# Eight-stage transformer kernel on one core: stage joints' transposes placed further back, tail weights in buffers of their own, and the end of the convolution stage rearranged

## The chip, the cores and the metric

The kernel runs on one core of one Trainium2 chip. The metric is device microseconds (us) of one execution, the median of several runs. The engines are named as in the profile: PE is TensorE, DVE VectorE, ACT ScalarE, POOL GpSimd, and SP the engine that only issues transfers here.

## The reference, cut to what matters

Two blocks work on one sequence of 256 tokens with 1024 features in fp32. Each has two mixers, and a SwiGLU feed-forward part behind each mixer: eight stages of the form `x = x + f(rms_norm(x))`.

```python
def rms_norm(x, w):
    xf = x.astype(jnp.float32)
    y = xf * lax.rsqrt(jnp.mean(xf * xf, axis=-1, keepdims=True) + NORM_EPS)
    return (y * w.astype(jnp.float32)).astype(x.dtype)
...
def swiglu(h, w_gate, w_up, w_down):
    return (jax.nn.silu(h @ w_gate) * (h @ w_up)) @ w_down
...
def conformer_conv(h, w_pw1, b_pw1, w_dw, b_dw, ln_g, ln_b, w_pw2, b_pw2):
    a, gate = jnp.split(h @ w_pw1 + b_pw1, 2, axis=-1)
    u = a * jax.nn.sigmoid(gate)
    dw = lax.conv_general_dilated(
        u, w_dw[:, None, :], window_strides=(1,), padding=((CONV_WIDTH_2 - 1, 0),),
        dimension_numbers=('NWC', 'WIO', 'NWC'), feature_group_count=D_MODEL) + b_dw
    d32 = dw.astype(jnp.float32)
    mu = jnp.mean(d32, axis=-1, keepdims=True)
    var = jnp.mean(jnp.square(d32 - mu), axis=-1, keepdims=True)
    z = (d32 - mu) * lax.rsqrt(var + EPS) * ln_g + ln_b
    z = jax.nn.silu(z).astype(h.dtype)
    return z @ w_pw2 + b_pw2
```

The mixers are, in order, a state-space and gated-linear-attention layer, a latent attention (called mla), a retention layer with pooling, and the convolution stage above (conformer), with 31 taps for each feature.

## The kernel before

**Precision.** Each fp32 product is made of three: every operand is split in a part `hi` (a cast, on ACT) and a rest `lo` (a subtraction, on DVE), and PE adds hi by hi, hi by lo and lo by hi. `load` does this for a piece of weights: fetch `raw` by DMA, four casts (L159), four subtractions (L160). `split` does it for activations (L164 on ACT, L165 on DVE).

**A stage.** `x` lies as two tiles of 128 tokens, t0 and t1. The last step of a stage is `outproj`: it takes weights in chunks of two times 128 rows, and keeps the last two chunks as a tail that it runs in four groups of 12 matmuls of 512 columns: t0 first half, t0 second half, t1 first half, t1 second half. When a group is done, DVE adds it to `x` (L382) and ACT squares that half (L274). After the second half of a tile DVE, POOL (`r`, a power of -1/2, L227) and DVE again (`xn`, L291) make the normed tile, PE transposes it in eight 128 by 128 pieces (`transposes`, L251), ACT casts the transpose from PSUM to `xT` hi (L164), and DVE subtracts for `xT` lo (L165). The next stage multiplies by `xT`.

**Joints.** The passage from one stage to the next is called a joint here; there are seven, 1 to 7. Code is written stage by stage, and a scheduler sets each engine's order by priorities: `high_priority(offset=FIRST)` brings an instruction forward, `issue_after` holds it behind another. In a joint PE runs the transposes of t0 inside the last group of the old stage, and those of t1 inside the first matmuls of the new stage, which work on t0's tokens.

**The convolution stage (joint 6 to joint 7).** `proj(i)` makes four slices of the gated input, `conv(ks)` the taps. Most taps run on PE: for each tap and 128 features two diagonal matrices (hi and lo) are made by ACT (`diags`, L1095: identity times a column of the weights `whl_dw`), and three matmuls of 256 columns (L311 to L313) use them. The other taps run on DVE. Then follow, for all features, the statistics (`stat`: transposes L1204, bn_stats, bn_aggr), POOL's power (`lnr`, L1225), eight broadcast matmuls in PSUM (L1229), a multiply and an add on DVE (L1235, L1236), SiLU on ACT, a split to `zTh` and `zTl`, and `outproj` with `conv_w_pw2`, whose bias `bp` is added to `x` on DVE (L1242).

Of the kernel before, what the change touches and what calls it, by code (L numbers as in the profile page):

```python
# [17 lines left out]
P = 128  # L18
D = 1024
# [38 lines left out]
class Net:  # L58
    def __init__(self, tc, a, ctx):
# [3 lines left out]
        self.entry = []  # L63
        pool = lambda name, bufs, **kw: ctx.enter_context(tc.tile_pool(name=name, bufs=bufs, **kw))
# [81 lines left out]
    def load(self, srcs, k, n, ahead=None, pieces=None, raw=None):  # L146
# [61 lines left out]
    def warm(self, n):  # L208

        b = self.bank("pw", (P, P))  # L210
        for i in range(n):
            self.nc.tensor.matmul(b, self.ones, self.ones, start=True, stop=True)
# [83 lines left out]
    def norm_T(self, t, gain, xn=None, ssq=None):  # L296
        xn = self.normed(t, gain, xn, ssq)
        self.last_norm = self.rs.ins
        self.transposes(xn, self.xT[0][:, :, T(t)], self.xT[1][:, :, T(t)], D)
        self.last_xT = self.last_hi, self.last_lo  # L300


    def mm3A(self, out, lh, ll, wh, wl, first, last):
        mm = self.nc.tensor.matmul
        mm(out, lh, wh, start=first, stop=False)  # L305
        mm(out, lh, wl, start=False, stop=False)  # L306
        mm(out, ll, wh, start=False, stop=last)  # L307
# [13 lines left out]
    def projA(self, w, evac, n=512, tok=(0, 1)):  # L321
# [4 lines left out]
        for t in tok:  # L326
            b = self.bank("acc")
            for k in range(8):
                hi, lo = ch[k // kc]
                self.mm3A(b[:, :n], xh[:, k, T(t)], xl[:, k, T(t)], hi[:, k % kc, :], lo[:, k % kc, :], k == 0, k == 7)  # L330
# [14 lines left out]
    def outproj(self, w, lhs, ks, after, tail=2, ahead=None, pieces=None):  # L345
# [5 lines left out]
        def mms(c, t, hi, lo, hs=(0, 1)):  # L351
            for j in range(2):
                lh, ll = lhs(ks[2 * c + j], t)
                st, sp = c == 0 and j == 0, c == nch - 1 and j == 1
                for h in hs:
                    cs = slice(h * 512, h * 512 + 512)
                    b = banks[t][h]
                    nc.tensor.matmul(b, lh, hi[:, j, cs], start=st, stop=False)  # L358
                    nc.tensor.matmul(b, lh, lo[:, j, cs], start=False, stop=False)  # L359
                for h in hs:  # L360
                    cs = slice(h * 512, h * 512 + 512)
                    nc.tensor.matmul(banks[t][h], ll, hi[:, j, cs], start=False, stop=sp)  # L362
# [994 lines left out]
```

## Time and profile before

| | |
|---|---|
| median of 3 runs | 1308.64 us (1308.57 to 1309.65) |
| profiled execution | 1307.43 us |
| its span, first to last instruction | 1305.4 us |
| PE busy | 1272.3 us, 97% of the span |
| DVE busy | 913.7 us, 70% |
| ACT busy | 780.6 us, 60% |
| POOL busy | 47.7 us, 4% |
| mean granted PE clock | 0.995 |

The span is 2.0 us shorter than the profiled execution's time: that much lies before the first and behind the last instruction. The profiled execution is 1.2 us below the median. A time in a row of the trace counts from the start of the span. A busy share is an average over stages that are limited in different ways, so the sections below go by stretches.

### The profile page before, as it was taken

How to read it: one execution, taken by the hardware profiler on the slowest of the kernel's cores; microseconds unless marked ns; L12 is line 12 of the kernel's file. 1: busy time of each engine (PE TensorE's matmuls, PEld its weight loads, DVE VectorE, ACT ScalarE, POOL GpSimd, SP SyncE). 2: the span in 40 equal slices, each digit the busy share in tenths (PEclk: the TensorE clock that was granted, in tenths of full speed). 3: DMA queues.
4: the chain of work that ended last, by engine and by line, in shares of the span. 5: the costliest groups of instructions: out<-in, count | busy, mean ns of one | idle time of the engine just before them, and what ended most of it. 6: DMA issues, size and time to landing. Idle time of an engine off the chain costs nothing.

```text
span 1305.4 us, 19252 instructions
## 1 busy us (share of the span) xinstructions
PE 1272.3 (97%) x7148; PEld 1090.7 (84%) x7148; DVE 913.7 (70%) x1884; ACT 780.6 (60%) x1794; POOL 47.7 (4%) x103
## 2 busy tenths in 40 slices
PE   9999999999999999999999999999999997999997
PEld 8888877888888867888887887888889996888886
DVE  6966666777746887866746787776548997776643
ACT  6773554666644876666644445666439995666642
POOL 3000000300000000000000000000000000000000
PEclk9999999999999999999999999999999998999999
DMA  8436344766553432766554545555665204555561
GB/s 251 144 119 208 129 181 148 221 194 194 194 193 137 166 97 87 237 194 194 194 194 163 202 137 190 179 181 179 220 194 163 88 11 156 183 182 179 188 220 38
DMA packets 150543, 219.62 MB, mean 168 GB/s; under 512 B 6634, under 2 KB 119426, under 8 KB 150450
## 3 DMA queue, kind: packets, MB, share of 16 engines
q1 hardware_dynamic: 148528, 213.43, 50.4%
q0 software_dynamic: 1920, 4.96, 1.4%
q8 instruction: 56, 0.92, 0.3%
q14 instruction: 37, 0.30, 0.1%
q10 hardware_dynamic: 2, 0.00, 0.0%
HBM read 217.33 MB, written 1.05 MB: 167 GB/s over the span
## 4 chain that ended last, share of the span: by engine, by line
PE 86%; DVE 7%; ACT 3%; issue 2%; POOL 1%; DMA 1%; POOLq 0%; DVEq 0%; ACTq 0%
PE acc L318 18%; PE acc L319 9%; PE acc L358 8%; PE acc L359 8%; PE acc L362 8%; PE pw L318 5%; PE acc L307 4%; PE acc L305 4%; PE acc L306 4%; DVE lo L160 3%; PE pw L319 2%; PE acc L313 2%; PE acc L312 2%; PE acc L311 2%; PE ptr L251 2%
## 5 line engine op out<-in xcount | busy, mean ns | idle before, releaser
L160 DVE TENSOR_TENSOR lo<-raw,hi 128x512 fp32r<-128x512 f32 (+2 forms) x800 | 515.7, 683 | 194.8 <-ACT hi L159 192.5
L159 ACT CAST hi<-raw 128x512 fp32r<-128x512 f32 (+2 forms) x800 | 448.8, 616 | 247.4 <-PE acc L362 101.1
L318 PE MATMUL acc<-xT,hi 128*128 128x512 f32 x1024 | 361.6, 398 | 0.0
L319 PE MATMUL acc<-xT,lo 128*128 128x256 f32 x1024 | 287.6, 281 | 0.0
L318 PEld LDWEIGHTS acc<-xT,hi 128*128 128x128 f32 x1024 | 192.3, 188 | 46.7
L319 PEld LDWEIGHTS acc<-xT,lo 128*128 128x128 f32 x1024 | 193.4, 189 | 0.2
L359 PE MATMUL acc<-lo,hTh 128*128 128x512 f32 x352 | 137.3, 390 | 0.0
L358 PE MATMUL acc<-hi,hTh 128*128 128x512 f32 x352 | 137.3, 390 | 0.0
L362 PE MATMUL acc<-hi,hTl 128*128 128x512 f32 x352 | 113.6, 389 | 0.0
L305 PE MATMUL acc<-hi,xT 128*128 128x512 f32 (+2 forms) x288 | 108.3, 376 | 0.0
L307 PE MATMUL acc<-hi,xT 128*128 128x512 f32 (+2 forms) x288 | 108.0, 375 | 0.0
L306 PE MATMUL acc<-lo,xT 128*128 128x512 f32 (+2 forms) x288 | 107.7, 374 | 0.0
L423 DVE TENSOR_TENSOR s<-s,acc 128x256 f32<-128x256 f32 x128 | 53.3, 417 | 52.7 <-ACT s L422 52.6
L318 PE MATMUL pw<-xT,hi 128*128 128x512 f32 x256 | 90.2, 397 | 0.0
L313 PE MATMUL acc<-xT,lo 128*128 128x256 f32 x288 | 81.9, 284 | 0.0
L311 PE MATMUL acc<-xT,hi 128*128 128x256 f32 x288 | 81.8, 284 | 0.0
L312 PE MATMUL acc<-xT,hi 128*128 128x256 f32 x288 | 81.8, 284 | 0.0
L358 PEld LDWEIGHTS acc<-hi,hTh 128*128 128x128 f32 x352 | 66.1, 188 | 13.7
L362 PEld LDWEIGHTS acc<-hi,hTl 128*128 128x128 f32 x352 | 66.1, 188 | 13.6
L359 PEld LDWEIGHTS acc<-lo,hTh 128*128 128x128 f32 x352 | 66.1, 188 | 13.6
L422 ACT COPY s<-acc 128x256 f32<-128x256 f32 x128 | 47.3, 370 | 45.2 <-PE acc L319 45.2
L319 PE MATMUL pw<-xT,lo 128*128 128x256 f32 x256 | 71.8, 281 | 0.0
(429 smaller groups left out, 2003.6 us busy)
## 6 DMA issues: line engine op xcount, KB each, us to landing
raw<-w_in_even SPq DMA_DIRECT2D x22, 1024.0 KB, 5.3
raw<-w_down SPq DMA_DIRECT2D x22, 1024.0 KB, 5.0
raw<-ffn_w_down SPq DMA_DIRECT2D x22, 1024.0 KB, 5.0
raw<-w_gate SPq DMA_DIRECT2D x20, 1024.0 KB, 5.4
raw<-w_up SPq DMA_DIRECT2D x20, 1024.0 KB, 5.4
raw<-ffn_w_gate SPq DMA_DIRECT2D x20, 1024.0 KB, 5.3
raw<-ffn_w_up SPq DMA_DIRECT2D x20, 1024.0 KB, 5.4
raw<-conv_w_pw SPq DMA_DIRECT2D x12, 1024.0 KB, 5.2
```

What stands on the lines that cost most here:

```text
L159: nc.scalar.copy(fl(hi)[:, c], fl(raw)[:, c])
L160: nc.vector.tensor_sub(fl(lo)[:, c], fl(raw)[:, c], f32(fl(hi)[:, c]))
L305: mm(out, lh, wh, start=first, stop=False)
L306: mm(out, lh, wl, start=False, stop=False)
L307: mm(out, ll, wh, start=False, stop=last)
L311: mm(out, wh, xh, start=first, stop=False)
L313: return mm(out, wl, xh, start=False, stop=last).ins
L318: mm(out.rearrange("p a s -> p (a s)"), wh, self.xx[:, k].rearrange("p a s -> p (a s)"), start=first, stop=False)
L319: mm(out[:, 0, :], wl, self.xx[:, k, 0, :], start=False, stop=last)
L358: nc.tensor.matmul(b, lh, hi[:, j, cs], start=st, stop=False)
L359: nc.tensor.matmul(b, lh, lo[:, j, cs], start=False, stop=False)
L362: nc.tensor.matmul(banks[t][h], ll, hi[:, j, cs], start=False, stop=sp)
```

## The change

**Joints.** `norm_T` now returns a function that does the transposes. `outproj` calls it for t0 behind the fourth matmul of the last group (`done[3]`), and leaves t1's to the next stage, which calls it in `second` behind its 23rd of 24 matmuls on t0 (feed-forward and retention stages), its 40th of 48 (mla) or its 44th of 48 (conformer). The casts of the two loads that follow are held behind the joint (`self.hold`).

**Own tail buffers.** `own=True` in the two feed-forward stages ahead of mla and of the conformer puts the tail chunks' hi and lo into the stage's own pool, so that the buffers of the common pool `whl` are free for the next stage's weights before the joint.

**Convolution stage.** The split of the tap weights `whl_dw` moves behind the joint. The 16 diagonals of the first eight taps of the last 128 features (k = 7) are made by one POOL instruction. Products on a constant matrix of ones, whose results nobody reads, run after the last statistics transposes (`warm(10, "ptr")`) and after the broadcast matmuls (`warm(7, "ptr")`). Of the output weights' pieces the first four casts come ahead of ACT's last 20 diagonals, and DVE's subtractions for the next are held behind given steps.

```diff
-    def load(self, srcs, k, n, ahead=None, pieces=None, raw=None):
+    def load(self, srcs, k, n, ahead=None, pieces=None, raw=None, pool=None):
...
-        hi = self.whl.tile([P, k, n], F32R, tag="hi", name="hi")
-        lo = self.whl.tile([P, k, n], F32R, tag="lo", name="lo")
-        with self.tc.high_priority(offset=ahead):
+        hi, lo = [(pool or self.whl).tile([P, k, n], F32R, tag=t, name=t, bufs=2 if pool else None) for t in ("hi", "lo")]
+
+        whole, parts = self.hold.pop(0) if self.hold else ((), ())
+        with self.tc.high_priority(offset=ahead), ExitStack() as st:
+            for ins in whole:
+                st.enter_context(self.tc.issue_after(ins))
...
-                nc.vector.tensor_sub(fl(lo)[:, c], fl(raw)[:, c], f32(fl(hi)[:, c]))
+                with self.tc.issue_after(parts[i]) if parts else nullcontext():
+                    nc.vector.tensor_sub(fl(lo)[:, c], fl(raw)[:, c], f32(fl(hi)[:, c]))
...
+    def behind(self, ins, turn):
+
+        with self.tc.high_priority(offset=FIRST), self.tc.issue_after(ins):
+            turn()
+
+    def second(self, mms, n):
+
+        if self.turn_xT:
+            self.behind(mms[min(n, len(mms)) - 1], self.turn_xT)
+            self.turn_xT = None
+
+            self.joint = self.last_hi, self.last_lo
+            self.hold = [(self.joint, ())] * 2
...
-                after(t, xn, ssq)
...
+                turn = after(t, xn, ssq)
+            if t == 0:
+                turn0 = turn
+            elif turn:
+                self.behind(done[3], turn0)
+                self.turn_xT = turn
...
+                        self.second(mms, 23)
...
-            self.outproj(wd, lambda k, t: (hTh[:, k, T(t)], hTl[:, k, T(t)]), list(range(NC)), after)
+            self.outproj(wd, lambda k, t: (hTh[:, k, T(t)], hTl[:, k, T(t)]), list(range(NC)), after, pool=sp if own else None)
...
+                self.second(mms, 40)
...
+        if k == 7 and taps[0] == 0:
+
+            n = len(taps)
+            w = self.whl_dw[:, 0, :n, :, k].rearrange("p a b -> p (a b)").rearrange("p (a o) -> p a o", o=1).to_broadcast([P, 2 * n, P])
+            self.nc.gpsimd.affine_select(t[:, :2 * n], w, pattern=[[0, 2 * n], [1, P]], base=0, channel_multiplier=-1, compare_op=ALU.is_equal, fill=0.0)
+            return t
...
+                        self.second(mms, 44)
...
+                if ks[0] == 0:
+                    with self.tc.issue_after(self.joint[0]), self.tc.issue_after(self.joint[1]):
+                        for i in range(2):
+                            n = 16 - i
+                            self.split(self.whl_dw[:, i, :n, 0], self.whl_dw[:, i, :n, 1], self.wdw[:, i::2])
...
+                with self.tc.issue_after(turned):
+                    self.warm(10, "ptr")
...
+                with self.tc.issue_after(ins):
+                    self.warm(7, "ptr")
...
-            self.outproj(a["conv_w_pw2_2"][0], lambda k, t: (zTh[:, k, T(t)], zTl[:, k, T(t)]), list(range(8)), after, ahead=1)
+
+            self.hold = [((), ()), ((), (eps, eps, adds[1], adds[2])), ((), (adds[3],) * 4)]
+            self.outproj(a["conv_w_pw2_2"][0], lambda k, t: (zTh[:, k, T(t)], zTl[:, k, T(t)]), list(range(8)), after, ahead=1, ahead0=120)
```

How the order of instructions changes is shown at three places. A row is a line of the code, the operation, output and inputs, and the shape; `xN` is a number of equal instructions in a row.

PE in joint 1 before: the last group of the old stage is `acc<-..,mT`, the new stage's matmuls on t0 are `acc<-..,xT`.

```order
L359 MATMUL acc<-lo,mT_1477 128x512
L362 MATMUL acc<-hi,mT_1478 128x512
L251 MATMUL ptr<-ident,xn 128x128 x4
L358 MATMUL acc<-hi,mT_1477 128x512
L251 MATMUL ptr<-ident,xn 128x128 x4
L359 MATMUL acc<-lo,mT_1477 128x512
L362 MATMUL acc<-hi,mT_1478 128x512
...
L306 MATMUL acc<-lo,xT 128x512
L307 MATMUL acc<-hi,xT 128x512
L251 MATMUL ptr<-ident,xn 128x128 x8
L305 MATMUL acc<-hi,xT 128x512
L306 MATMUL acc<-lo,xT 128x512
```

The same place of the changed kernel:

```order
L389 MATMUL acc<-hi,mT_1478 128x512
L385 MATMUL acc<-hi,mT_1477 128x512
L258 MATMUL ptr<-ident,xn 128x128 x8
L386 MATMUL acc<-lo,mT_1477 128x512
L389 MATMUL acc<-hi,mT_1478 128x512
...
L330 MATMUL acc<-hi,xT 128x512
L330 MATMUL acc<-lo,xT 128x512
L258 MATMUL ptr<-ident,xn 128x128 x8
L331 MATMUL acc<-hi,xT 128x512
L330 MATMUL acc<-hi,xT 128x512
L330 MATMUL acc<-lo,xT 128x512
L331 MATMUL acc<-hi,xT 128x512
```

The transposes of t0 moved from the border of the last group to behind four of its 12 matmuls, and those of t1 from behind 18 to behind 23 of the new stage's 24 matmuls on t0, so that one of these is left behind them and t1's own matmuls follow.

ACT at the end of the convolution stage, before:

```order
L1173 CAST uh_10750<-uh 128x285
L1174 CAST ul_10751<-ul 128x285
L1095 ACTIVATE diag<-ident,whl_dw 128x128 x36
L159 CAST hi<-raw 128x512 x12
L1238 ACTIVATE d<-d,lp 128x256
L164 CAST zTh<-d 128x256
```

And of the changed kernel:

```order
L1140 ACTIVATE diag<-ident,whl_dw 128x128 x13
L164 CAST hi<-raw 128x512 x2
L1222 CAST uh_10750<-uh 128x285
L164 CAST hi<-raw 128x512
L1223 CAST ul_10751<-ul 128x285
L164 CAST hi<-raw 128x512
L1140 ACTIVATE diag<-ident,whl_dw 128x128 x20
L164 CAST hi<-raw 128x512 x8
```

Sixteen diagonals left ACT, and four of the twelve casts of output weights that stood behind the last diagonal stand ahead of the last 20.

DVE in joint 6, of the changed kernel; `xT` here is lo, `x_82` and `x_83` are t0 and t1 of `x`:

```order
L411 TENSOR_TENSOR x_83<-x_83,acc 128x512
L294 SCALAR_TENSOR_TENSOR v_9510<-ssq_9504,v_9509 128x1
L298 SCALAR_TENSOR_TENSOR xn<-x_83,r,gain 128x512 x2
L1298 TENSOR_TENSOR x_82<-x_82,bp 128x1024
L1298 TENSOR_TENSOR x_83<-x_83,bp 128x1024
L171 TENSOR_TENSOR xT<-ptr,xT 128x4x128 x2
L166 TENSOR_TENSOR lo<-raw,hi 128x512 x4
```

Before, the two adds of `bp` stood behind t1's `xT` and behind the subtraction for `whl_dw`; now they stand between t1's `xn` and its `xT`. The transfer of `bp`, on SP's queue, waits in both kernels for a matmul that last reads what lay in its place: before for one of the retention stage, now for the sixth matmul of the last group of the stage ahead (the second behind t0's transposes).

## Rows read from the trace of the kernel before

**Rows 1.** Page, part 1: busy time and share of the span by engine.

```profile
PE 1272.3 (97%) x7148; PEld 1090.7 (84%) x7148; DVE 913.7 (70%) x1884; ACT 780.6 (60%) x1794; POOL 47.7 (4%) x103
```

**Rows 2.** TensorE's waits over the span: us in total, times, longest.

```profile
PE ptr L251 <- DVE xn L291: 7.7, 16, 0.6
```

**Rows 3.** TensorE timeline, joint 1: start, duration, in brackets idle before.

```profile
217.49 0.39 PE L362 MATMUL acc<-hi,mT 128*128 128x512 f32 x1
217.72 0.39 PE L358 MATMUL acc<-hi,mT 128*128 128x512 f32 x1
...
219.82 0.63 PE L251 MATMUL ptr<-ident,xn 128*128 128x128 f32 x4 [0.58 <-DVE xn L291]
...
228.13 1.29 PE L251 MATMUL ptr<-ident,xn 128*128 128x128 f32 x8 [0.40 <-DVE xn L291]
```

**Rows 4.** VectorE timeline, joint 1.

```profile
221.11 0.69 DVE L165 TENSOR_TENSOR xT<-ptr,xT 128x512 fp32r<-128x512 f32 x1 [0.17 <-ACT xT L164]
...
223.02 1.29 DVE L160 TENSOR_TENSOR lo<-raw,hi 128x512 fp32r<-128x512 f32 x2
224.23 0.68 DVE L382 TENSOR_TENSOR x<-x,acc 128x512 f32<-128x512 f32 x1
```

**Rows 5.** GpSimd timeline, joint 6 and the end of the convolution.

```profile
978.67 0.56 POOL L227 TENSOR_TENSOR r<-v,nhalf 128x1 f32<-128x1 f32 x1 [176.60 <-DVE v L287]
...
1080.04 1.08 POOL L1225 TENSOR_TENSOR lnr<-rm,nhalf 128x2 f32<-128x2 f32 x1 [90.24 <-DVE rm L1224]
```

**Rows 6.** Windows: us, busy of each engine, TensorE clock, DMA share, GB/s.

```profile
988.00:1076.00 88.00, 87.59 (x714) 86.49 (x714) 83.19 (x196) 87.48 (x269) 0.58 (x1) 1.00 0.27 90
1069.00:1076.40 7.40, 7.40 (x48) 6.53 (x47) 4.75 (x13) 7.40 (x26) 0.00 (x0) 1.00 0.01 2
...
1081.00:1091.00 10.00, 7.30 (x20) 5.92 (x21) 8.96 (x19) 6.83 (x13) 0.12 (x1) 0.50 0.64 210
```

**Rows 7.** ScalarE timeline, joint 6.

```profile
987.43 0.49 ACT L164 CAST whl_dw<-wdw 128x128 fp32r<-128x128 f32 x2
987.83 0.98 ACT L1095 ACTIVATE diag<-ident,whl_dw 128x128 fp32r<-128x128 f32 x3
```

**Rows 8.** ScalarE timeline, end of the convolution.

```profile
1065.62 10.65 ACT L1095 ACTIVATE diag<-ident,whl_dw 128x128 fp32r<-128x128 f32 x36
1076.18 3.20 ACT L159 CAST hi<-raw 128x512 fp32r<-128x512 f32 x6
```

**Rows 9.** VectorE timeline, end of the convolution.

```profile
1076.74 0.42 DVE L1198 TENSOR_TENSOR d<-d,pw 128x256 f32<-128x256 f32 x1 [2.99 <-PE pw L313]
...
1078.54 0.63 DVE L160 TENSOR_TENSOR lo<-raw,hi 128x512 fp32r<-128x512 f32 x1
...
1083.29 0.42 DVE L1235 TENSOR_TENSOR d<-d,pw 128x256 f32<-128x256 f32 x1 [0.76 <-PE pw L1229]
1083.63 0.68 DVE L160 TENSOR_TENSOR lo<-raw,hi 128x512 fp32r<-128x512 f32 x1
```

**Rows 10.** TensorE timeline, end of the convolution.

```profile
1077.22 0.44 PE L1204 MATMUL ptr<-ident,d 128*128 128x128 f32 x2 [0.52 <-DVE d L1198]
1081.18 1.22 PE L1229 MATMUL pw<-ident,lnr 128*128 128x128 f32 x4 [3.52 <-POOL lnr L1225]
...
1085.77 0.80 PE L358 MATMUL acc<-hi,zTh 128*128 128x512 f32 x1 [2.52 <-ACT zTh L164]
1086.36 0.63 PE L359 MATMUL acc<-lo,zTh 128*128 128x512 f32 x1
1086.79 0.63 PE L358 MATMUL acc<-hi,zTh 128*128 128x512 f32 x1
```

**Rows 11.** DMA issues from 974 to 984: KB, median us from issue to landing.

```profile
bp<-conv_b_pw SPq DMA_DIRECT2D x1, 512.0 KB, 6.2
```

**Rows 12.** VectorE timeline: the two adds of the convolution's last bias.

```profile
992.24 2.35 DVE L1242 TENSOR_TENSOR x<-x,bp 128x1024 f32<-128x1024 f32 x2
```

**Rows 13.** TensorE timeline, start of the kernel: products on ones.

```profile
1.10 4.63 PE L212 MATMUL pw<-ones 128*128 128x128 f32 x20 [1.10 <-POOL ones L88]
```

More of the change, by code (lines that the diff above doesn't have):

```diff
@@ L1 @@
 import math
-from contextlib import ExitStack
+from contextlib import ExitStack, nullcontext
 import numpy as np
@@ L206, in load_x, with warm @@
         return gain
-    def warm(self, n):
-        b = self.bank("pw", (P, P))
+    def warm(self, n, tag="pw"):
+        b = self.bank(tag, (P, P))
         for i in range(n):
-            self.nc.tensor.matmul(b, self.ones, self.ones, start=True, stop=True)
+            ins = self.nc.tensor.matmul(b, self.ones, self.ones, start=True, stop=True).ins
+        return ins
     def gain(self, g, eng=None):
@@ L298, in norm_T, with turn @@
         self.last_norm = self.rs.ins
-        self.transposes(xn, self.xT[0][:, :, T(t)], self.xT[1][:, :, T(t)], D)
-        self.last_xT = self.last_hi, self.last_lo
+        xh, xl = self.xT
+        def turn():
+            self.transposes(xn, xh[:, :, T(t)], xl[:, :, T(t)], D)
+        return turn
+    def behind(self, ins, turn):
[4 more added lines that the diff above has]
+            self.behind(mms[min(n, len(mms)) - 1], self.turn_xT)
+            self.turn_xT = None
+            self.joint = self.last_hi, self.last_lo
+            self.hold = [(self.joint, ())] * 2
     def mm3A(self, out, lh, ll, wh, wl, first, last):
         mm = self.nc.tensor.matmul
-        mm(out, lh, wh, start=first, stop=False)
-        mm(out, lh, wl, start=False, stop=False)
-        mm(out, ll, wh, start=False, stop=last)
+        return [mm(out, lh, wh, start=first, stop=False).ins, mm(out, lh, wl, start=False, stop=False).ins,
+                mm(out, ll, wh, start=False, stop=last).ins]
     def mm3W(self, out, wh, wl, xh, xl, first, last):
@@ L343, in projW, with outproj @@
         return ins
-    def outproj(self, w, lhs, ks, after, tail=2, ahead=None, pieces=None):
+    def outproj(self, w, lhs, ks, after, tail=2, ahead=None, pieces=None, pool=None, ahead0=None):
         nc = self.nc
@@ L366, in outproj @@
             k0 = ks[2 * c]
-            hi, lo = self.load([w[k0 * P:(k0 + 2) * P, :]], 2, D, ahead, pieces=pieces if c < 2 else None)
+            hi, lo = self.load([w[k0 * P:(k0 + 2) * P, :]], 2, D, ahead0 if ahead0 and c == 0 else ahead, pieces=pieces if c < 2 else None, pool=pool if c >= nch - tail else None)
             if c < nch - tail:
@@ L1108, in conformer @@
             self.whl_dw = pp.tile([P, 2, 16, 2, 8], F32R, name="whl_dw")
-            for i in range(2):
-                n = 16 - i
-                self.split(self.whl_dw[:, i, :n, 0], self.whl_dw[:, i, :n, 1], self.wdw[:, i::2])
             with self.tc.issue_after(self.last_norm):
@@ L1180, in conv @@
                             ts = taps[odd][t0:t0 + 8]
-                            dg = self.diags(pp, ts, k)
+                            with self.tc.issue_after(self.joint[0]):
+                                dg = self.diags(pp, ts, k)
                             for n, tap in enumerate(ts):
@@ L1228, in conformer @@
                     for t in range(2):
-                        nc.tensor.matmul(br[:, i, T(t)], x[:, t, :].to_broadcast([P, P]), self.ident, start=True, stop=True)
-            k = 0
+                        ins = nc.tensor.matmul(br[:, i, T(t)], x[:, t, :].to_broadcast([P, P]), self.ident, start=True, stop=True).ins
+                with self.tc.issue_after(ins):
+                    self.warm(7, "ptr")
+            k, adds = 0, []
             for w in (1, 1, 2, 2, 2):
```

52 lines of the change are left out of this document (32 added, 20 removed).

## The prediction, made before the changed kernel ran

> **What bounds the kernel now.** I read the page's first part: TensorE is busy for 97% of the span, so time can only be won where it pauses, where it is paced by another engine, or where its clock is low [rows 1]. The view of its waits says where it pauses: the largest entry is its wait for the normed tile `xn` ahead of the transposes, 16 times, 7.7 us together [rows 2]. Two of these stand at the kernel's start with 1.0 us; the other 14 are the two pauses of each of the seven joints, 6.7 us or 0.48 us each. The slot lost is longer than the pause shown: a 512-column matmul is drawn 0.39 us long but the next starts after 0.227 us, so 0.16 us of each pause lies under the last matmul's drawn end [rows 3]. That makes 0.64 us a pause, 1.29 us a joint, 9.0 us in all. This is the most that the joints can give.
>
> The windows show a second place. From joint 6 to the last tap ScalarE is busy for 87.5 of 88.0 us, so this stretch is as long as ScalarE's list of work; TensorE looks as busy, but near the end its matmuls are spread out by the diagonals they wait for. After it, from 1081 to 1091, TensorE's granted clock is 0.50, its 1.2 GHz level, where it is 1.00 before [rows 6]. It fell after TensorE had waited 3.52 us for POOL's power, and stayed down while it waited 2.52 us more for `zTh` [rows 10].
>
> **Joints, t0.** The transposes come four matmuls later, 4 x 0.227 = 0.91 us, against a slot of 0.64 to 0.75 us that was lost (0.58 + 0.16 in joint 1) [rows 3]. `xn` is then there; I leave 0.05 us. What follows them, the new stage's first matmul on `xT`, comes 8 x 0.227 = 1.8 us behind the eight transposes, and the first half of `xT` lo is there 221.11 + 0.69 - 219.82 = 1.98 us after they start [rows 3, 4], against 1.0 + 1.8 = 2.8 us: no new wait.
>
> **Joints, t1.** With T the start of t0's transposes, TensorE reaches t1's at T + 1.0 (eight transposes) + 1.8 + 23 x 0.227 = T + 8.0. In joint 1 one subtraction of 0.64 us still stands ahead of t1's last add to `x`; this add then starts at about 3.2 + 0.64 = T + 3.8 (223.02 less 219.82 and one of the two subtractions), and from its start to the transposes before it were 228.13 - 224.23 = 3.9 us [rows 3, 4]: ready at T + 7.7, or T + 8.2 if ScalarE's square waits behind a cast. I take 0.1 us of pause, bounds 0 and 0.3. A new wait follows: only one matmul of t0 is left behind t1's transposes, and t1's third matmul wants `xT` lo at 1.0 + 3 x 0.227 = 1.7 us, when it is there after 1.98 us. So 0.3 us, bounds 0.1 and 0.8 (the chain on ScalarE and VectorE late by a subtraction). Behind the waiting matmul stands the whole queue of TensorE.
>
> A joint so gives 1.29 - 0.05 - 0.1 - 0.3 = 0.84 us (bounds 0.3 and 1.2); five of them (1, 3, 4, 5, 7) 4.2 us. In joint 2 (mla) eight matmuls are left behind t1's transposes, and with own tail buffers no subtraction stands in the chain: 1.2 us. Sum 5.4 us. Joint 6 gives nothing, since ScalarE bounds what follows.
>
> **Joint 6 to the last tap.** ScalarE's list behind joint 6 changes as follows. Sixteen diagonals go to POOL, but three were made inside the joint before [rows 7], so 13 x 0.296 = 3.8 us less (10.65 us for 36); eight casts more (four of a load that is now held behind the joint, four of the output weights ahead of the last 20 diagonals), 8 x 0.533 = 4.3 us (3.20 us for six) [rows 8]; and the split of `whl_dw`, 0.45 us of 0.49 [rows 7]. The last diagonal comes 0.9 us later. Bounds: 0, if ScalarE finds its half microsecond of idle time and joint 6 ends earlier; 2.6 with the next paragraph.
>
> The adds of `bp`, 2.35 us [rows 12], now stand on VectorE ahead of t1's `xT` lo. Their transfer waits for the second matmul behind t0's transposes, T + 1.0 + 0.45, and landed 6.2 us after issue before [rows 11]: T + 7.65. The adds then last to T + 10.0. T1's transposes come at T + 1.0 + 1.8 + 44 x 0.114 = T + 7.8 (a 256-column matmul at half of 0.227), and `xT` lo would start 1.3 us later, at T + 9.1 [rows 3, 4]. TensorE waits some 0.9 us for it. ScalarE next needs TensorE's result behind eight held casts, the `whl_dw` split and some diagonals, over 5 us, so I cost this at nothing; if the transfer lands 1.7 us later still, that cover is gone, and 1.7 us goes onto the chain.
>
> **POOL's diagonals.** No row shows so wide a select. Below, nothing: POOL has idled for 90 us ahead of its power [rows 5]. Above, as slow as ScalarE's sixteen, 4.7 us, hidden while they are asked for late. I take nothing. POOL's power took 0.56 us with VectorE idle and 1.08 us with subtractions beside it [rows 5]. The Trainium skill, "SBUF — State Buffer", section "Who interferes with whom", says that a VectorE instruction with two SBUF inputs and a GpSimd instruction that reads SBUF lock each other out for a whole instruction; the two durations agree. By that rule VectorE would stand still for the whole select; the rival below prices this.
>
> **End of the convolution.** VectorE's subtractions between the two bn_aggr and the epsilon go, 2 x 0.54 us from start to next start (0.63 us long): 1.1 us. The broadcast matmuls took from 1081.18 to VectorE's multiply at 1083.29, 2.1 us at the lower clock; at the upper half of that: 1.05 us. The subtraction between the first multiply and add (0.68 us, 0.6 to the add) goes [rows 9, 10]. The output projection so starts 2.7 us earlier after the last tap. Its matmuls start every 0.43 us, against 0.227, until about 1091.1: 13 of them, 13 x 0.20 = 2.6 us [rows 3, 10]. Together 5.3 us; less 0.9 us by which the last tap is late: 4.4 us. All that rests on the clock rests on the products on ones. Ten took 4.63 us at the start of the kernel [rows 13], at the lower level; half of that, 2.3 us, fits the pause, which is 1.1 us shorter than 3.52 now. Bounds: all 5.3 us, and -1.4 us (first rival). The Trainium skill, "TensorE: Matmul & The Clock Gate", Part 1, says that the gate looks at recent activity and that the lower clock is the default; this trace agrees (0.50 behind the pause), but whether products on a constant count as activity here no row shows beyond the kernel's start.
>
> **Sum.** 5.4 + 4.4 = 9.8 us off the profiled execution's 1307.43 us: 1297.6. That execution is 1.2 us below the median of 1308.64 us, to which the forecast is put: **1298.8 us**.
>
> **Rivals.**
> - *The clock falls all the same* (TensorE also waits about 2 us for the last 20 diagonals, behind the four casts). The ten products then last 4.63 us from 1077.7 to 1082.3, the broadcast ends at 1084.4, 1.1 us behind that of before; less 0.6 us for the subtraction. With the 0.9 us: -1.4 us, total 5.4 - 1.4 = 4.0: 1304.6. For it: it fell here before. Against: ten products fill the wait.
> - *T1's transposes only turn into waits for `xT` lo*, 0.8 us in five joints instead of 0.3 and 0.1: 2.0 us less, 1300.8; with the `bp` transfer late too, 1302.5. For it: one matmul of cover. Against: with the loads held, VectorE has nothing else to do there.
> - *Slower: the stretch of taps turns into lock-step.* TensorE and ScalarE are both full there, with 0.5 us of slack [rows 6]. The changed order puts taps between projection matmuls; if a tap waits for a late diagonal, the projections behind it wait too, and with them the sigmoids that ScalarE needs. Eight groups of features hand over so; from 9.8 / 8 = 1.2 us each the whole gain is gone, and at 1.6 us it is 1311.8. Against: ScalarE sets that pace already.
> - *POOL's select locks VectorE out* for up to 4.7 us at the end; 2.99 us idle ahead of its last add cover most [rows 9]: 1.7 us, 1300.5.
> - *The change doesn't do what it says*: new waits of equal size at the joints, 1308.
>
> **How the numbers follow.** Forecast 0.60 (own range 1296 to 1301.5); clock 0.16; `xT` lo 0.10; lock-step 0.07; POOL 0.03; nothing 0.04. A measurement of this kernel tells about 0.2%, 2.6 us, from no change. Faster than 1306.0: 0.60 + 0.10 + 0.03 + nine tenths of the clock's = 0.87; the same: 0.02 + 0.04 = 0.06; slower 0.07. The range goes from 1294.8 (full gain at most pauses, last tap not late) to 1305 (the clock's case).
>
> **What would show it.** Right: at the joints the wait for `xn` falls from 7.7 us to under 2.5; a short wait for `xT` lo behind t1's transposes; granted clock 1.00 through the end of the convolution, output matmuls 0.227 us apart from the first; the last tap 0.9 us later after joint 6. Wrong: a window at 0.50 behind the last tap, TensorE idle between projections of the convolution stage, or a wait for `bp` on VectorE beyond 1 us.

## The result and the profile after

The changed kernel took 1294.03 us (median of 4 runs, 1290.46 to 1296.40) against 1308.61 us: ratio 0.9889, 95% interval 0.9874 to 0.9905, 14.6 us faster. The forecast was 1298.8 us in a range from 1294.8 to 1305.0: the direction was right, and the time lies 0.8 us below the range. The profiled execution took 1293.72 us, with a span of 1292.0 us.

TensorE's waits, in the view and columns of [rows 2], some of its lines:

```profile
PE pw L335 <- ACT diag L1140: 1.3, 1, 1.3
...
PE ptr L594 <- DVE acp L591: 1.3, 1, 1.3
...
PE acc L385 <- ACT zTh L170: 0.5, 1, 0.5
...
PE ptr L258 <- DVE xn L298: 0.4, 1, 0.4
...
PE pw L1282 <- POOL lnr L1278: 0.3, 1, 0.3
...
PE acc L331 <- DVE xT L171: 0.2, 1, 0.2
```

The wait for `xn` fell from 7.7 us to 0.4, and that one is at the start of the kernel: no joint has one any more. POOL's power is waited for 0.3 us instead of 3.5. Waits for a diagonal (1.3 us here, and 0.5 at another line) are new. `acp`, a tile of the first mixer, was waited for longer before:

```profile
PE ptr L558 <- DVE acp L555: 2.8, 1, 2.8
```

TensorE's timeline at joint 1, answering to [rows 3]; behind t1's transposes their one matmul of t0 and the first three of t1:

```profile
218.71 1.12 PE L258 MATMUL ptr<-ident,xn 128*128 128x128 f32 x8
...
226.75 1.16 PE L258 MATMUL ptr<-ident,xn 128*128 128x128 f32 x8
227.66 0.47 PE L331 MATMUL acc<-hi,xT 128*128 128x512 f32 x1
228.02 0.50 PE L330 MATMUL acc<-hi,xT 128*128 128x512 f32 x1
228.36 0.39 PE L330 MATMUL acc<-lo,xT 128*128 128x512 f32 x1
228.75 0.50 PE L331 MATMUL acc<-hi,xT 128*128 128x512 f32 x1
```

Before, behind t1's transposes at 228.13 [rows 3]:

```profile
229.18 0.48 PE L305 MATMUL acc<-hi,xT 128*128 128x512 f32 x1
229.49 0.39 PE L306 MATMUL acc<-lo,xT 128*128 128x512 f32 x1
```

T1's transposes start 8.04 us after t0's, when TensorE gets there. The third matmul of t1, which wants `xT` lo, starts 0.39 us behind the second, and the matmuls around it are late too: four spacings from 227.66 on take 1.43 us (to 229.09), where they took 1.01 before (229.18 to 230.19). So the wait that the prediction put at 0.3 us is about 0.4 us, most of it drawn under the matmul before it. Against that, the transposes themselves got faster: the next matmul starts 0.91 us behind t1's first transpose, 1.05 before.

TensorE at the end of the convolution, answering to [rows 10]:

```profile
1069.80 0.44 PE L1254 MATMUL ptr<-ident,d 128*128 128x128 f32 x2 [0.51 <-DVE d L1248]
1070.08 2.40 PE L218 MATMUL ptr<-ones 128*128 128x128 f32 x20
1072.79 0.71 PE L1282 MATMUL pw<-ident,lnr 128*128 128x128 f32 x4 [0.31 <-POOL lnr L1278]
1073.33 0.61 PE L1282 MATMUL pw<-ident,rm 128*128 128x128 f32 x4
1073.78 1.73 PE L218 MATMUL ptr<-ones 128*128 128x128 f32 x14
1075.98 0.50 PE L385 MATMUL acc<-hi,zTh 128*128 128x512 f32 x1 [0.47 <-ACT zTh L170]
1076.32 0.40 PE L386 MATMUL acc<-lo,zTh 128*128 128x512 f32 x1
1076.55 0.39 PE L385 MATMUL acc<-hi,zTh 128*128 128x512 f32 x1
```

The output matmuls are 0.23 us apart from the second on (0.43 before). The rows of L218 are the products on ones, two for each product. The windows say why; columns as in [rows 6]:

```profile
1069.00:1073.00 4.00, 3.17 (x27) 2.78 (x25) 2.49 (x9) 3.97 (x8) 1.11 (x1) 1.00 0.02 7
1073.00:1076.00 3.00, 2.53 (x23) 2.34 (x22) 2.48 (x6) 1.08 (x3) 0.00 (x0) 1.00 0.00 0
1076.00:1082.00 6.00, 6.00 (x26) 4.96 (x27) 5.87 (x12) 5.47 (x11) 0.00 (x0) 1.00 0.00 0
```

The granted clock stays at 1.00, the 2.4 GHz level, where it was 0.50. From the last tap to the first output matmul 6.97 us pass (1069.01 to 1075.98) instead of 9.39, and from there to the next stage's first matmul 23.03 instead of 26.24.

What the sum does not hold shows when the trace is cut at the first matmul of each stage on its new `xT`, on TensorE's timeline (times in us; the last stretch ends with TensorE's last matmul):

| stretch | before | after | gain |
|---|---|---|---|
| to joint 1 | 223.49 | 221.52 | 1.97 |
| feed-forward 1 | 186.83 | 185.80 | 1.03 |
| mla | 107.28 | 105.34 | 1.94 |
| feed-forward 2 | 187.73 | 186.69 | 1.04 |
| retention | 90.69 | 89.70 | 0.99 |
| feed-forward 3 | 187.74 | 184.62 | 3.12 |
| convolution | 128.25 | 125.34 | 2.91 |
| feed-forward 4, to the end | 186.31 | 185.89 | 0.42 |

Joints give about 1.0 us a stretch. The first stretch holds a wait for `acp` that fell from 2.8 to 1.3 us in a part of the program that is the same in both kernels. And the third feed-forward stage gained 2.1 us more than its neighbours, and no wait inside the stage had shrunk. Its projections are pairs of matmuls, of 512 columns (hi) and 256 (lo). Before, ten pairs:

```profile
875.61 0.40 PE L318 MATMUL acc<-xT,hi 128*128 128x512 f32 x1
875.85 0.28 PE L319 MATMUL acc<-xT,lo 128*128 128x256 f32 x1
...
879.14 0.40 PE L318 MATMUL acc<-xT,hi 128*128 128x512 f32 x1
```

After, in the same place:

```profile
867.77 0.39 PE L342 MATMUL acc<-xT,hi 128*128 128x512 f32 x1
868.00 0.28 PE L343 MATMUL acc<-xT,lo 128*128 128x256 f32 x1
...
871.23 0.39 PE L342 MATMUL acc<-xT,hi 128*128 128x512 f32 x1
```

Ten pairs take 3.53 us before and 3.46 after. Over the stage the mean pair is 0.3533 us and 0.3467 us; 320 pairs make the 2.1 us. The whole difference lies between the start of hi and the start of lo (0.2367 and 0.2300 us); from lo to the next hi it is 0.1167 us in both. In the other stages nothing like it had changed in this pair of traces.

### The profile page after: what moved, and what is told of

Read it like the earlier page. It is cut to its first block, busy times and chain, and to the rows that moved or that the text cites. A ratio compares the mean times of both kernels' runs of the same rounds, so it can differ in the third digit from the quotient of the medians.

```text
span 1292.0 us, 19321 instructions
## 1 busy us (share of the span) xinstructions
PE 1271.6 (98%) x7182; PEld 1094.1 (85%) x7182; DVE 913.5 (71%) x1884; ACT 774.7 (60%) x1778; POOL 49.4 (4%) x104
## 3 DMA queue, kind: packets, MB, share of 16 engines
HBM read 217.33 MB, written 1.05 MB: 169 GB/s over the span
## 4 chain that ended last, share of the span: by engine, by line
PE 89%; DVE 6%; ACT 3%; issue 1%; DMA 0%; POOL 0%; POOLq 0%; DVEq 0%; ACTq 0%
PE acc L342 18%; PE acc L343 9%; PE acc L330 9%; PE acc L385 9%; PE acc L389 9%; PE acc L386 9%; PE pw L342 5%; PE acc L331 5%; PE pw L343 2%; PE acc L337 2%; PE acc L336 2%; PE acc L335 2%; PE ptr L258 1%; DVE lo L166 1%; ACT hi L164 1%; PE pw L335 1%
```

## The experiments

Every run was timed against the kernel before on the same chip, in five rounds; ratios are given with their 95% intervals. "Pace" is the mean time of a pair in a feed-forward stage, worked out from starts on TensorE's timeline.

**The two kernels once more** (`before_again`, `after_again`, later `after_third`), unchanged.

> The kernel before, unchanged, to see what differs from one execution to the next. In the two profiles so far, the program up to joint 1 has the same order of instructions on TensorE and VectorE, yet the wait for acp was 2.77 us before and 1.25 us after; and in the third feed-forward stage a pair of projection matmuls (512 and 256 columns) took 0.3534 us before and 0.3467 after, 2.1 us over the stage. Theory A (these 3.6 us are of the execution, not of the change): in this profile one or both take another value than in the first one, the wait below 2.0 us or the pair away from 0.3534. Theory B (the change made them, by other addresses of its tiles): 2.7 to 2.9 us and 0.353 to 0.354 again.

> The changed kernel, unchanged. Theory A: the wait for acp or the pair of the third feed-forward stage takes another value than 1.25 us and 0.3467 us, and the ratio over five rounds comes nearer to 0.991 to 0.993 (the joints and the convolution's end alone, about 9.3 us in the profiles). Theory B: 1.25 and 0.3467 again, ratio 0.989.

Before: 1.0005 [0.9996, 1.0013]; pace 0.3533 in stages two to four again, the wait for `acp` 2.24 us. After: 0.9904 [0.9891, 0.9918], pace 0.3533, 0.3467, 0.3533 again, `acp` 1.34. 2.24 us lies between what the two theories said of `acp`, and 1.34 is near theory B's 1.25, so nothing was settled there yet; for the pace theory A seemed to fall.

**Joints alone, convolution alone** (`joints_only`, `conv_only`).

```diff
 joints_only: -  the two warm() calls, the POOL diagonals, self.hold and ahead0 of the convolution;
              +  whl_dw split at the head of its stage, diagonals not behind self.joint
 conv_only:   -  self.behind(done[3], turn0); self.turn_xT = turn; own=True
              +  turn()
```

> The joints' part alone with own tail buffers: the convolution stage keeps its products of before (no products on ones, diagonals on ScalarE, whl_dw split at its head, output weights not held or brought forward). By the profiles the joints gave about 1.0 us each, 7.0 us in all, of which joint 6 is lost again if ScalarE bounds what follows: 1300.5 to 1302.5 (ratio 0.9938 to 0.9954). By the prediction as written 5.4 us: 1303.2. Theory B adds 2 us: 1298.5 to 1300.5.

> The convolution stage's part alone: transposes at the joints where they were, no own tail buffers. By the prediction 5.3 us less 0.9 of lateness: 1304.2, the sixth joint as before. By the profile of the changed kernel, where the last tap came 2.7 us later after the stage's start and the rest gave 5.0 us: 2.3 to 3.5 us, 1305.1 to 1306.3 (ratio 0.9973 to 0.9982). Theory A has no other gain; theory B (own tail buffers or the joints moved tiles) has none here either.

0.9903 [0.9888, 0.9918], 1294.73 us; and 0.9979 [0.9971, 0.9988], 1303.62 us. The joints' part alone is as fast as the whole change: the forecast of 4.4 us for the convolution is not there on top of it. In its trace the convolution stage is 1.9 us shorter too, which the prediction did not give to the joints. The convolution's part alone was a little faster than both of its expectations. In the joints' kernel the third feed-forward stage has the pace 0.3467, in the convolution's 0.3533.

**Own tail buffers** (`no_own`, `own_only`, `own_all`).

```diff
 no_own:   -own=True (both stages)
 own_only: the kernel before with +own=True in both stages
 own_all:  -def ffn(..., own=False)
           +def ffn(..., own=True)
```

> The changed kernel with own=False in both feed-forward stages: tail weights in the common pool as before. In three profiles with own buffers a pair of projection matmuls of the third feed-forward stage took 0.3467 us, in three without 0.3533. Theory B (own buffers, by where tiles lie or when casts run): 0.3533 again, 2.1 us back, and some of joints 2 and 6 too: 1296.5 to 1298. Theory C (the pair follows the joints' moved transposes, through the place of instructions): 0.3467 stays, 1294 to 1295.5.

> The kernel before with own tail buffers alone, in the two feed-forward stages of the change: transposes and the convolution stage as before. Theory B: pair 0.3467 in the third feed-forward stage, 2.1 us, so 1304.5 to 1305 (ratio 0.998). Theory C: no pair but 0.3533 there and no change, 1306.5 to 1307.5.

> The changed kernel with own=True in all four feed-forward stages. If own buffers make the pair faster wherever they are (theory B in its simplest form): 0.3467 also in the second and fourth feed-forward stages, 2 x 2.1 us, about 1290. If the pair goes by something else that the change moved only in the third stage: 0.3533 in those two, 1293 to 1295; what own buffers do for a joint by themselves (the next stage's casts before it) is at most 0.4 us each.

0.9946 [0.9925, 0.9966]; 0.9981 [0.9967, 0.9995]; 0.9906 [0.9887, 0.9925]. Theory B fell: `own_only` has 0.3533 in stages two to four, `no_own` 0.3467, 0.3467, 0.3533, `own_all` 0.3533, 0.3533, 0.3467. Theory C, in its simple form, fell with `own_all`: its joints are the changed ones and its third stage is slow. The buffers' own worth lies elsewhere. With the changed joints, mla took 108.90 us without them and 105.34 with, and the convolution stage 126.26 against 125.34. In the kernel before they change nothing in mla (107.23 against 107.28), and their 2.5 us is the convolution stage: 125.96 instead of 128.25, with the last tap 2.9 us earlier. In that trace the eight casts of weights that ScalarE makes between t0's and t1's `xT` before are gone from there, and the split of the tap weights and the first diagonals take their place (from 981.24 on, 987.43 before). Nor are own buffers free: in `own_all` the retention stage, behind one of the two stages that got them in addition, took 91.44 us instead of 89.70.

**The products on ones** (`no_warm`).

```diff
-                    self.warm(10, "ptr")
-                    self.warm(7, "ptr")
```

> The changed kernel without the 17 products on ones at the end of the convolution. If the products hold the clock: the granted clock behind the last tap falls to 0.50 as before, 13 output matmuls start 0.43 us apart (2.6 us) and the broadcast takes 2.1 us instead of 1.05: 1297 to 1298. If the shorter wait (subtractions out of the chain) was enough by itself: clock 1.00 and 1293.5 to 1294.5.

0.993 [0.9911, 0.9948], 1297.49 us. Its windows behind the last tap:

```profile
1070.00:1073.00 3.00, 0.46 (x5) 0.45 (x5) 2.29 (x8) 2.74 (x6) 1.11 (x1) 1.00 0.00 0
1073.00:1076.00 3.00, 0.96 (x8) 0.77 (x7) 2.48 (x7) 1.31 (x3) 0.00 (x0) 0.60 0.00 0
1076.00:1082.00 6.00, 6.00 (x18) 4.74 (x19) 5.87 (x12) 5.03 (x10) 0.00 (x0) 0.63 0.00 0
```

The clock falls here too (0.60 and 0.63 are means over stretches at both levels), and the convolution stage takes 127.45 us instead of 125.34. It falls later than before, though, behind the broadcast matmuls:

```profile
1072.56 0.71 PE L1280 MATMUL pw<-ident,lnr 128*128 128x128 f32 x4 [2.54 <-POOL lnr L1276]
```

They take 0.71 us here, as with the products, and 1.22 before [rows 10]; from the last tap to the first output matmul 6.97 us pass in both kernels. So in this pair of traces the shorter chain alone brought the broadcast to the upper level, and the products are what held it for the output matmuls: 2.1 us.

**Which part of the convolution's costs** (`joints_warm`, `no_early`, `no_pool`, `no_whl`).

```diff
 joints_warm: joints_only +self.warm(10, "ptr") +self.warm(7, "ptr")
 no_early:    -ahead=1, ahead0=120)
              +ahead=1)
 no_pool:     -        if k == 7 and taps[0] == 0:
              +        if False:
 no_whl:      +whl_dw split at the head of its stage, -issue_after(self.joint[0]) of the diagonals
```

> The joints' part with own buffers and, of the convolution's part, the products on ones alone: diagonals on ScalarE, whl_dw split at the stage's head, output weights neither held nor brought forward. In the traces the convolution stage took 125.34 us with the whole change, 127.45 without the products, 126.38 with none of its part. If the rest of its part costs more on ScalarE's list than it gives at the end: 124.2 to 125.0 us there, total 1293.0 to 1293.8. If it gives: 125.5 or more, 1294 to 1295.

> The changed kernel with the first output weights' casts no longer ahead of ScalarE's last 20 diagonals. If these four casts delay the last tap by their 2.1 us (TensorE waited 1.27 us for a diagonal there): the last tap comes 1.3 to 2.1 us earlier, and the casts then stand behind it, where the chain of the statistics leaves room: 1292.3 to 1293.0. If they are needed early, the first output matmul waits for them: 1294 or more. The prediction put 2.1 us of the last tap's delay on them.

> The changed kernel with the sixteen diagonals of the last features made by ScalarE again. If ScalarE bounds the stretch from joint 6 to the last tap: 16 x 0.296 = 4.7 us later, 1297.5 to 1299. If lock-step with TensorE bounds it instead: less than 2 us, 1294 to 1296.

> The changed kernel with the split of whl_dw at the head of its stage again and the diagonals not held behind the joint. In the trace of the changed kernel ScalarE stood idle for 3.9 us ahead of t1's xT in joint 6, and 1.5 and 3.0 us earlier in it, with nothing to do that was not held. If the hold costs what the prediction overlooked: ScalarE makes diagonals in these gaps, and the convolution stage takes about 123.9 us (122.85 without held and early output weights too, 1.04 for the early ones) instead of 125.35. If not: 125.2 to 125.5.

Ratios: 0.9878 [0.9863, 0.9894]; 0.9895 [0.988, 0.9911]; 0.9926 [0.9913, 0.9939]; 0.9906 [0.9889, 0.9923]. Most of these intervals overlap, so the parts are read from the traces, one of each kernel. The convolution stage repeats well there: 125.33 to 125.37 us in the five profiles that have its changed form and the changed joints, buffers and products in full (`after`, `after_again`, `after_third`, `own_all`, `nudge`), 128.25 and 128.53 in the two of the kernel before. From its first matmul, cut as above:

| kernel | last tap | to the first output matmul | rest | stage |
|---|---|---|---|---|
| before | 92.62 | 9.39 | 26.24 | 128.25 |
| changed | 95.34 | 6.97 | 23.03 | 125.34 |
| conv_only | 92.28 | 9.60 | 23.73 | 125.61 |
| own_only | 89.74 | 10.01 | 26.21 | 125.96 |
| joints_only | 91.55 | 9.41 | 25.42 | 126.38 |
| joints_warm | 91.56 | 8.54 | 23.04 | 123.14 |
| no_early | 93.20 | 8.07 | 23.03 | 124.30 |
| no_pool | 99.07 | 7.02 | 23.05 | 129.13 |
| no_whl | 90.05 | 11.01 | 23.04 | 124.10 |
| best (below) | 90.02 | 9.80 | 23.03 | 122.85 |

Holding the tap weights and diagonals behind the joint delays the last tap by 5.3 us (95.34 less 90.05), the early output weights by 2.1; POOL's diagonals win 3.7 us back, which is what `no_pool` loses. Put on top of the 91.55 of `joints_only`, the three give 95.25, and 95.34 was measured. The parts do not add up over the stage, however: `conv_only` and `own_only` shorten it by 2.6 and 2.3 us, each alone, and the whole change by 2.9. ScalarE in joint 6, in the changed kernel:

```profile
975.05 0.63 ACT L281 ACTIVATE xn<-x 128x512 f32<-128x512 f32 x1 [1.46 <-DVE x L411]
...
979.66 1.07 ACT L170 CAST xT<-ptr 128x512 fp32r<-128x512 f32 x2 [3.89 <-PE ptr L258]
980.62 2.19 ACT L164 CAST hi<-raw 128x512 fp32r<-128x512 f32 x4
```

and in `no_whl`:

```profile
976.81 0.50 ACT L170 CAST whl_dw<-wdw 128x128 fp32r<-128x128 f32 x2
977.26 0.70 ACT L1140 ACTIVATE diag<-ident,whl_dw 128x128 fp32r<-128x128 f32 x2
...
979.01 4.49 ACT L1140 ACTIVATE diag<-ident,whl_dw 128x128 fp32r<-128x128 f32 x15
983.41 1.04 ACT L170 CAST xT<-ptr 128x512 fp32r<-128x512 f32 x2
```

With the hold ScalarE stands idle for 1.5 us ahead of t1's last square and for 3.9 us ahead of t1's `xT`; without it the split of the tap weights and 17 diagonals fill these gaps. The hold is this dear only with the changed joints: `conv_only` has it too, but there eight casts of weights still run inside the joint, ScalarE stands idle for 1.55 us ahead of t1's `xT`, and the last tap comes 0.3 us earlier than before. That `no_whl` wins only 1.2 of the 5.3 us has its own reason, on TensorE:

```profile
1069.60 0.44 PE L1251 MATMUL ptr<-ident,d 128*128 128x128 f32 x2 [1.83 <-DVE d L1245]
1070.65 0.44 PE L1251 MATMUL ptr<-ident,d 128*128 128x128 f32 x2 [0.62 <-DVE d L1245]
1071.09 4.04 PE L218 MATMUL ptr<-ones 128*128 128x128 f32 x20
```

```profile
1071.00:1074.00 3.00, 3.00 (x15) 2.94 (x14) 2.21 (x8) 0.00 (x0) 1.11 (x1) 0.50 0.00 0
```

The taps on VectorE are last now, TensorE waits for them, and its clock is 0.50 in the window from 1071 to 1074 (the last line, columns as in [rows 6]). The ten products take 4.04 us instead of 2.40, and the broadcast waits behind them. This is the prediction's first rival at work, in another kernel. It is at work in `conv_only` too: its ten products take 3.67 us, behind a wait of 1.84 us for VectorE, at a mean clock of 0.51 from 1078 to 1081.

**What sets the pace** (`nudge`, `before_nudge`). The first feed-forward stage has three transposes of parameter columns in its fifth group of projections, two between pairs and one of 44 columns between hi and lo of a pair. Its pairs take 0.353 or 0.347 ahead of them and 0.3467 behind them in every trace. A trio of the same sizes from a constant, whose results nobody reads, was put in the third group of stages two to four:

```diff
+                            if nudge and (g, j, i) == (2, 0, 0) and k in (2, 5):
+                                def turn(ms=(120, 128) if k == 2 else (44,)):
+                                    for m in ms:
+                                        b = self.bank("ptr", (P, P))
+                                        nc.tensor.transpose(b[:, :m], self.onesd[:m, :], self.ident[:m, :m])
+                                self.behind(both[1 if k == 2 else 0], turn)
```

> The changed kernel with three useless transposes of a constant (120, 128 and 44 columns), whose results nobody reads, inside the third group of projections in feed-forward stages two to four; the first stage has such a trio already, and in every trace so far its pairs of 512- and 256-column matmuls take 0.3467 us behind it, whatever they took ahead of it. Theory D (a stage's pairs have two paces, 0.3467 and 0.3533, and keep the one in which the stretch was last entered): the second and fourth stages change from 0.3533 to 0.3467 behind the trio, 2 x 250 pairs x 0.0067 = 3.3 us less 0.7 us for nine transposes and their disturbance: 1291.0 to 1292.0. Theory B (it goes by where the tiles lie): no pair changes, 1294.5 to 1295.

> The kernel before with the trio of useless transposes in feed-forward stages two to four and nothing else. Theory D (two paces, set by how the stretch is entered): its pairs take 0.3533 us ahead of the trio and 0.3467 behind it in all three stages, 3 x 210 pairs x 0.0067 = 4.2 us less about 1.5 us that the three trios take: 1303.8 to 1304.8. If the pace goes with the joints' moved transposes alone: no pair changes, 1308 to 1308.5.

0.99 [0.988, 0.992], 1292.53 us, a little over the expected 1291.0 to 1292.0; and for the kernel before 0.9972 [0.9959, 0.9986], 1304.05 us, as expected. In both all three stages have 0.3467 behind the trio; ahead of it `before_nudge` has 0.3533 in all three. The trio's own cost is in the stage times: 184.6 us for the third feed-forward stage when it is fast throughout, 185.4 to 185.5 with a trio behind a slow start, 186.7 when it is slow throughout. `before_nudge` shortens its three stages by 1.3 us each in the trace, 3.9 us together, and its time by 3.7 us (1.8 to 5.4): instructions whose results nobody reads made the kernel faster. Its third feed-forward stage on TensorE's timeline, ten pairs ahead of the trio and ten behind it:

```profile
814.89 0.40 PE L318 MATMUL acc<-xT,hi 128*128 128x512 f32 x1
...
818.43 0.40 PE L318 MATMUL acc<-xT,hi 128*128 128x512 f32 x1
...
818.79 0.38 PE L425 MATMUL ptr<-ident,onesd 120*128 120x120 f32 x2
...
820.03 0.26 PE L425 MATMUL ptr<-ident,onesd 44*128 44x44 f32 x1
820.22 0.38 PE L319 MATMUL acc<-xT,lo 128*128 128x256 f32 x1
...
821.14 0.39 PE L318 MATMUL acc<-xT,hi 128*128 128x512 f32 x1
...
824.61 0.39 PE L318 MATMUL acc<-xT,hi 128*128 128x512 f32 x1
```

Ten pairs take 3.54 us ahead of the trio and 3.47 behind it.

> The changed kernel a third time. Theory D': with the changed place of the transposes of h (between the two matmuls of a pair) each execution enters the pace by chance: the third feed-forward stage, fast in the first two profiles, or the second or fourth, slow in both, may change. If the pace belongs to the program: 0.3533, 0.3467 and 0.3533 in stages two to four a third time.

0.9902 [0.9879, 0.9925], 1295.91 us. Its pace is 0.3467, 0.3533, 0.3533 in stages two to four, not 0.3533, 0.3467, 0.3533, and 0.347 ahead of the first stage's own trio where the earlier two had 0.353. One program takes another pace in another execution: theory D'. Its wait for `acp` is 3.1 us, where the same program had 1.3 twice: theory A for that one.

**Together** (`best`, `best44`): joints, own buffers, products on ones, POOL's diagonals, and the trio, or one transpose of 44 columns between hi and lo in the second group instead.

> The joints with own buffers, the products on ones, POOL's diagonals, and the trio in feed-forward stages two to four; whl_dw split at the head of its stage, output weights neither held nor brought forward. In the traces POOL's diagonals were worth 3.8 us and the convolution stage took 123.14 us without them. If both add up: 119.5 to 121 us there, and with the fast pace behind the trio 1286 to 1288. If TensorE or the joint bounds that stretch by now: 122.5 to 123.2 us and 1289 to 1290.5.

> The same with one useless transpose of 44 columns between the two matmuls of a pair in the second group, in place of the trio in the third. If this one, between hi and lo, sets the fast pace: 0.3467 behind it in stages two to four, 0.3 to 0.5 us a stage less than with the trio. If the pace stays what it was ahead of it: some stages at 0.3533, 1 to 3 us more than with the trio.

`best`: 0.9866 [0.9845, 0.9887], 1289.35 us, 4.7 us under the changed kernel's 1294.03, with intervals that overlap. Its convolution stage gained almost nothing from POOL's diagonals (122.85 against 123.14): the last tap comes 1.5 us earlier, but TensorE then waits 1.1 us for taps on VectorE, so the output matmuls start only 0.3 us earlier. `best44`: 0.9882 [0.9863, 0.9901]; all three stages stay at 0.3533. One transpose between hi and lo does not change the pace; which of the other two does, or their order, stays open.

## Why the prediction was wrong, step by step

**What bounds the kernel: the step that failed.** Waits, the paced stretch and the clock were read rightly. But the prediction held that time can only be won in those three places, and so put stretches in which TensorE is busy at its upper clock at nothing. In the profile 2.1 us of the 13.7 came from just there, from the pace of matmul pairs that wait for nothing, and over the profiles it is about 2.6 us on average (below).

How far the time missed the range is in part the draw of the executions. The three timings of the changed kernel gave 1294.03, 1294.12 and 1295.91 us, the last of them inside the range, and ratios of 0.9889, 0.9904 and 0.9902. The forecast's 9.8 us and the mean 2.6 us of the pace make 12.4 us, an estimate from the traces here, against 12.5 and 12.8 us by the second and third ratio. The 1.2 us that the prediction added to get from the profiled execution to the median was such a draw too: the changed kernel's median lies 0.3 us above its profiled execution, and the kernel before, timed five times more, had medians of 1306.8 to 1307.7.

**The sum against the trace.** Joints 1 to 5, with t0's part of joint 6 and both of joint 7, gave 7.5 us where 5.4 were forecast: 0.45 in the first stretch without `acp` (1.97 less 1.52), 1.0, 1.9 (with joint 2), 1.0, 1.0, 1.0 in the third feed-forward stage without the pace, and 1.1 at joint 7 (0.65 for t0 by the slot of [rows 3], 0.42 in the last stretch). The convolution stage gave the rest of its 2.91 us, 2.3, where 4.4 were forecast. That is 9.8 us, the forecast, by two errors that cancelled: luck. The other 3.6 us are the wait for `acp` (1.5) and the pace (2.1), and both were in no step of it; 0.3 us of the profiled 13.7 lie outside TensorE's stretches and stay open.

**Joints.** The mechanism was right: both pauses gone, a small wait for `xT` lo instead. What stays was put at 0.45 us a joint and is about 0.3 net: the pauses went whole, where 0.15 us was left for them, the wait is about 0.4 us instead of 0.3, and the faster transposes give 0.14 back (joint 1). Most of the 2.1 us over the forecast came from elsewhere. By the starts in the traces, an estimate, joint 6's t0 gave 0.7 us and was counted as nothing, and joint 2 gave 0.4 us more than its 1.2; mla's wait for `c` also fell, from 2.0 to 1.5 us.

**Joint 6 to the last tap: the term of the chain that was mis-sized.** The prediction added up ScalarE's list (13 diagonals less, eight casts more) and got 0.9 us later. The last tap came 2.7 us later after the stage's start. A list of work is the length of a stretch only if its engine can start on it: holding the diagonals behind the joint left ScalarE idle for 3.9 us there, and the hold stood in the diff. The list also left out what own tail buffers move ahead of the stage, 2.9 us of the last tap in `own_only`. `bp` behaved: its transfer landed after 3.6 us instead of 6.2, the adds ran at 978.03 and `xT` lo followed at 980.30, a wait of 0.2 us on TensorE.

**The end of the convolution.** Right in size: 2.42 us from the last tap to the first output matmul (2.7 forecast), and 3.21 behind it, which is the 2.6 us for 13 matmuls at the upper clock and joint 7's t0. That all of the clock's gain rests on the products was too much: `no_warm` loses 2.1 us, all of it behind the first output matmul, and keeps the faster broadcast: 1.19 us from its first matmul to VectorE's multiply, as with the products, and 2.11 before.

**Rivals.** The clock did not fall here, but did in `no_whl` and `conv_only`. Lock-step came only as 1.8 us of waits for diagonals. POOL's select cost nothing in time, but the lock is there:

```profile
1044.34 2.01 POOL L1135 TENSOR_SCALAR_AFFINE_SELECT diag<-whl_dw 128x2048 fp32r<-128x2048 f32 x1 [65.35 <-PE pw L337]
```

```profile
1044.84 2.18 DVE L1245 SCALAR_TENSOR_TENSOR d<-u,wdw,d 128x256 f32<-128x256 f32 x2
...
1047.31 0.87 DVE L1245 SCALAR_TENSOR_TENSOR d<-u,wdw,d 128x256 f32<-128x256 f32 x2
```

Two such instructions take 0.87 us, and 2.18 beside the select, which was done at 1046.35: the first of the two took 1.78 us, the second its usual time. The Trainium skill, "SBUF — State Buffer", section "Who interferes with whom", says that a VectorE instruction with two SBUF inputs and a GpSimd instruction that reads SBUF exclude each other; the trace agrees, at 1.3 us, in a place where VectorE was not waited for. Which engine loses differs: in `best` the select came into a row of such instructions on VectorE that had begun before it, and has 7.44 us in the trace, while these kept their 0.40 us from start to start for 5.9 us:

```profile
1039.82 7.44 POOL L1141 TENSOR_SCALAR_AFFINE_SELECT diag<-whl_dw 128x2048 fp32r<-128x2048 f32 x1 [62.18 <-PE pw L337]
```

The prediction's own two durations show less than it took from them, since the 0.56 us is of one column and the 1.08 us of two; at one column the power took 0.55 us alone and 0.87 beside a subtraction (226.33 in the trace before).

**The pace: the term that was missing.** In all five profiles with the old place of t1's transposes (`before`, `before_again`, `conv_only`, `own_only`, and `before_nudge` ahead of its trio) the pairs were entered at 0.353 in all four stages, 20 of 20. In the 14 with the new place they were entered at 0.347 in 20 of 56. What moved at that spot: the transposes of `h` (t0), which were between two pairs and now stand between hi and lo of one. So the change gave, on average over executions, about 2.4 us in stages two to four (16 of 42 entries, 3 stages of 2.1 us) and 0.2 in the first. That the pace is a state that lasts until something disturbs it is shown by the trio; that the place of `h`'s transposes is what makes the entry a toss is the reading that fits all 19 profiles, but `h` alone was not moved. What the state is, the traces do not tell; they place it between hi and lo of a pair.

The wait for `acp` went from 1.1 to 3.1 us over the 19 profiles, of programs that have the same order of instructions up to there, so no part of the change made it.

## What to carry to other kernels

Where an engine bounds a stretch, add up not only its work but the times at which it may start on it: a hold that keeps casts out of a chain can leave the engine idle that bounds the next stretch. A busy TensorE has a pace too: compare the spacing of equal matmuls between stages and executions before calling a stretch full. Where gains of single parts do not add up, as in the convolution stage here, time the parts alone as well as leaving each out. And when a traced gain exceeds the sum, cut both traces at the same instructions first; here two wrong terms cancelled, and only the cut showed it.

## What the runs showed that was not expected

Pairs of a 512- and a 256-column matmul in a steady stream ran at 0.3467 or 0.3533 us, each kept until something disturbed it, without a wait in either. A trio of transposes (120, 128 and 44 columns) left the pairs behind it at 0.3467 in 28 of 28 places (19 in the first stage, 9 in the others); a single one of 44 columns changed nothing in 3 of 3.
